# An in-order load queue and accumulating DMA for the weight sums of a Strassen-like up-projection

## The chip, the cores and the metric

One core of a Trainium2 chip runs the whole kernel. The metric is the device time of one execution in microseconds (us), lower is better. TensorE (PE) multiplies, VectorE (DVE) and ScalarE (ACT) prepare operands and take results away, GpSimd (POOL) here does nothing but issue transfers, and SyncE (SP) issues most loads and stores. Each engine works through its own list of instructions in order; waits between engines and transfers are semaphores.

## The reference, cut to what matters

One layer of a decoder on 512 tokens of width 2048, in float32: sliding-window attention with sinks, then a gated feed-forward network with a causal convolution of width 3. The change lies in the second part:

```python
u = h @ w_up                       # 512 x 2048 by 2048 x 11264
c = conv_w[0] * up[:, 0:S] + conv_w[1] * up[:, 1:1 + S] + conv_w[2] * up[:, 2:2 + S]
gate, val = jnp.split(c, 2, axis=-1)
return (jax.nn.silu(gate) * val) @ w_down      # 512 x 5632 by 5632 x 2048
```

## The kernel before, in words

Every float32 operand is split in two float32r halves, high and low: ACT copies the tile to `wh` (line 64), DVE subtracts that from the tile to get `wl` (line 65). Each product is then three matmuls (`prod`, line 83 records them all): high by high, high by low, low by high.

The up-projection works on the 44 column blocks of 128 gate columns and the 128 value columns that belong to them. Blocks 0 to 3 are done in the plain way. Blocks 4 to 43 are done by `up_pair(f)`, in which a 2 by 2 product costs seven block products in place of eight (Winograd's form of Strassen's method). The four weight blocks of a pair, `b11`, `b21`, `b12`, `b22` (512 KB each), come through `block` (line 656) into the pool `bw` of six buffers. DVE forms sums of them in the tile `t` (named `raw`; lines 681, 688, 692, 695). Each of the seven products is 8 x 3 = 24 matmuls of 128x256, so one pair has 168. The order of the products is 2, 7, 5, 6, 3, 1, 4; product 2 needs `b11 + b21`. After the last product ACT copies the result from PSUM (line 704), `gate` does the convolution (lines 567 to 569), SiLU (574) and the gating product (576), and a store on the SP queue writes the activations of the block to the DRAM tensor `hd` (line 578).

The down-projection is also done with seven products. It needs sums of the weight blocks of `wdn`, kept in the DRAM tensor `td`: four sums for each of 22 pairs of blocks (`kp`). The first six are made earlier. The sixteen for `kp` 6 to 21 are made in the up-projection stage, in turn by two helpers that share four buffers `ts` of 512 KB: `weight_sums` (POOL issues four loads, line 141; DVE adds, line 144; POOL issues four stores, line 145) and `queue_sums` (POOL issues loads, line 151, transfers that add to what is in the buffer, line 152, and stores, line 153). Every fifth pair starts one of each kind.

In the down-projection `weight_form` loads 512 KB per step on the SP queue (line 768), from `td` or from `wdn`, into four buffers `raw`; `fetch` (line 555) brings the activations back from `hd`. Each step is 12 matmuls of 128x512, and there are 7 x 22 = 154 steps.

Order: matmuls are pinned to the order of the program text by `tc.keep_in_program_order`. That call orders an instruction behind the one that the text puts last before it on the same engine, whether that one is pinned or not; it sets the order of issue and waits for nothing to finish. All other instructions, the transfers on SP among them, are ordered by a scheduler that works from its own model of the times.

The text around the change reads, in `up_pair` and `gate`:

```python
b11, b21 = block(f, 0, 0), block(f, 1, 0)
...
gate(f, (ug, uv))
...
cv = conv_half(o[1], f, 1)
nc.vector.tensor_tensor(cv, cg, cv, ALU.mult)
nc.sync.dma_start(hd[:, par, :, kp, :].rearrange("m p t -> p m t"), ...)
```

Of the kernel before, what the change touches and what calls it, by code (L numbers as in the profile page):

```python
# [14 lines left out]
ALU = mybir.AluOpType  # L15
# [20 lines left out]
NP = NF // 2  # L36
# [5 lines left out]
def trunk(ctx, tc, xT, x, grow, table, onehot, masked, sinks, conv,  # L42
          wkv, wq, wo, wup, wdn, out):
    nc = tc.nc
# [12 lines left out]
    def bank(i):  # L57
        return ps.tile([P, 512], F32, name=f"b{i}", bufs=1)
# [4 lines left out]
    def split(hi, lo, src):  # L63
        nc.scalar.activation(hi, src, AF.Copy)  # L64
        nc.vector.tensor_tensor(lo, src, hi.bitcast(F32), ALU.subtract)  # L65

    def halves():
        p = ring["slots"][ring["next"] % len(ring["slots"])]
        ring["next"] += 1
        return p.tile([P, 1024], F32R, name="wh"), p.tile([P, 1024], F32R, name="wl")  # L70
# [64 lines left out]
    hd = dr.tile([2, 2, P, NP, HALF], F32, name="hd")  # L135
    td = dr.tile([NP, P, 4, 1024], F32, name="td")

    def weight_sums(kp, sums):
        t = [sums.tile([P, 1024], F32, name="ts") for _ in range(4)]
        for q in (0, 2, 1, 3):  # L140
            nc.gpsimd.dma_start(t[q], wdn[4 * kp + q])
        yield
        for q, o in ((2, 0), (0, 1), (1, 2), (3, 1)):
            nc.vector.tensor_tensor(t[q], t[q], t[o], ALU.add)  # L144
            nc.gpsimd.dma_start(td[kp, :, q, :], t[q])
            yield

    def queue_sums(kp, sums):
        t = [sums.tile([P, 1024], F32, name="ts") for _ in range(4)]
        for q, other in ((2, 0), (0, 1), (1, 2), (3, 1)):  # L150
            nc.gpsimd.dma_start(t[q], wdn[4 * kp + q])
            nc.gpsimd.dma_start(t[q], wdn[4 * kp + other] if q in (0, 2) else t[other], accum_op=ALU.add)
            nc.gpsimd.dma_start(td[kp, :, q, :], t[q])

    def step(g, n=1):
        for _ in range(n):
            next(g, None)

    with ExitStack() as att:
# [10 lines left out]
        with ExitStack() as ph:  # L170
# [26 lines left out]
            for kt in range(KT):  # L197
                if kt == 0:
                    for h in range(2):
                        r = first[:, KT:] if h == 0 else pa.tile([P, 512], F32, name="xs")  # L200
                        c = KT + h * S
                        nc.sync.dma_start(r if h else first, xT[:, c if h else 0:c + S])
                        if h == 0:
                            w = halves()
                            raw = wraw.tile([P, 1024], F32, name="raw")
# [4 lines left out]
                elif kt % 2 == 0:  # L210
                    r = pa.tile([P, 1024], F32, name="xr")
# [205 lines left out]
        for u in range(NKV * NT):  # L417
            t = Unit(u)
# [28 lines left out]
    with ExitStack() as op:  # L447
        sums = op.enter_context(pool("tso", 4))
# [5 lines left out]
        g1 = gp.tile([P, D], F32, name="g1")  # L454
# [42 lines left out]
        def oproj(d, o):  # L497
            for u in range(8):
                w = weights(wo, 8 * d + u)
                for b in range(NT):  # L500
                    for k in range(2):
                        kt = 2 * u + k
                        prod(o[b], station(b, kt), wide(w, k), kt == 0, kt == KT - 1)
                if u % 4 == 0:
                    g = weight_sums(2 * d - 2 + u // 4, sums)
                step(g, (1, 0, 2, 3)[u % 4])
            for b in range(NT):
                evac_m(b, d, o[b])
# [9 lines left out]
        for b, bk in enumerate((2, 5, 6, 7)):  # L518
            o = bank(bk)
            for kt in range(KT):  # L520
                prod(o, station(b, kt), wide(ws[kt // 2], kt % 2), kt == 0, kt == KT - 1)
                if b > 1:
                    turn_tok(b - 2, kt, (0, 1, 3, 4))
                if b < 2:
                    if kt == 0:
                        g = weight_sums(4 + b, sums)
                    if kt in (0, 9, 11, 13, 15):
                        step(g)
            evac_m(b, 3, o)
            xn[b] = finish_tok(b)  # L530

        wu = {(h, u): weights(wup, 2 * h + u) for h in range(4) for u in range(2)}
        o = [bank(k) for k in (0, 1, 2, 5)]
# [18 lines left out]

    def fetch(m, par, g0, g1):
        t, k0 = next((t, k) for t, k, k1 in hq[m, par] if k <= g0 < k1)
        nc.sync.dma_start(t[:, g0 - k0:g1 - k0, :], hd[m, par, :, g0:g1, :])

    with ExitStack() as us:
        fp = us.enter_context(pool("fp", 1))
# [13 lines left out]
        def gate(f, o):  # L572
            cg = conv_half(o[0], f, 0)
            nc.scalar.activation(cg, cg, AF.Silu)
            cv = conv_half(o[1], f, 1)
            nc.vector.tensor_tensor(cv, cg, cv, ALU.mult)
            kp, par = divmod(f, 2)
            nc.sync.dma_start(hd[:, par, :, kp, :].rearrange("m p t -> p m t"),
                              cv.rearrange("p (m t) -> p m t", m=2))
# [72 lines left out]
        sums = tsu.enter_context(pool("tsu", 4, side="right"))  # L652

        def block(f, r, c):
            t = bw.tile([P, 1024], F32, name="bw")
            nc.sync.dma_start(t, wup[4 * f + 2 * c + r])
            return t

        def form(t):
            w = halves()  # L660
            split(*w, t)
            return w

        def times(o, n, w, fresh):
            o3 = o[:, :HALF].rearrange("p (a b) -> p a b", a=2)
            a = forms[n]
            for k in range(8):
                prod(o3, cols(w, k), tuple(v[:, :, k, :] for v in a), fresh and k == 0, k == 7, not fresh)

        def shot(o, name):  # L670
            t = un.tile([P, HALF], F32, name=name)
            nc.scalar.activation(t, o[:, :HALF], AF.Copy)  # L672
            return t

        def up_pair(f, g):
            X, Y, Z = (bank(k) for k in ((0, 1, 6), (3, 4, 7))[f % 2])
            ug = un.tile([P, S], F32, name="ug", bufs=2)
            uv = un.tile([P, S], F32, name="uv", bufs=2)
            b11, b21 = block(f, 0, 0), block(f, 1, 0)
            t = wraw.tile([P, 1024], F32, name="raw")  # L680
            nc.vector.tensor_tensor(t, b11, b21, ALU.add)
            times(X, 2, form(t), True)
            s1 = shot(X, "s1")
            step(g)
            b12 = block(f, 0, 1)
            times(Z, 7, form(b12), True)
            s7 = shot(Z, "s7")
            nc.vector.tensor_tensor(t, t, b12, ALU.add)
            times(X, 5, form(t), False)
            s2 = shot(X, "s2")  # L690
            step(g)
            nc.vector.tensor_tensor(b11, b11, b12, ALU.add)
            times(Z, 6, form(b11), False)
            b22 = block(f, 1, 1)
            nc.vector.tensor_tensor(t, t, b22, ALU.add)
            times(X, 3, form(t), False)
            s3 = shot(X, "s3")
            step(g)
            nc.vector.tensor_tensor(ug[:, :HALF], Z[:, :HALF], s2, ALU.subtract)
            times(Y, 1, form(b21), True)  # L700
            nc.vector.tensor_tensor(uv[:, :HALF], s3, s7, ALU.subtract)
            times(X, 4, form(b22), False)
            nc.vector.tensor_tensor(ug[:, HALF:], s1, Y[:, :HALF], ALU.subtract)
            nc.scalar.activation(uv[:, HALF:], X[:, :HALF], AF.Copy, scale=-1.0)
            gate(f, (ug, uv))

        kp = 6
        for f in range(4, NF):
            i = f - 4
            if i % 5 == 0 and kp < NP:  # L710
                work = weight_sums(kp, sums)
                step(work)
                kp += 1
            up_pair(f, work if i % 5 == 1 else iter(()))
            if i % 5 == 1:
                step(work)
            if i % 5 == 1 and kp < NP:
                queue_sums(kp, sums)
                kp += 1
            if kp == NP and tsu:  # L720
                tsu.close()
                tsu = None
                early = ctx.enter_context(pool("early", 1, side="right"))
                hq[1, 0] = [(early.tile([P, 16, HALF], F32, name="hq10"), 0, 16)]
                for g0, g1 in batches[:4]:
                    fetch(1, 0, g0, g1)
# [38 lines left out]
    def weight_form(src, kp):  # L765
        raw = raws[kp % 2].tile([P, 1024], F32, name="raw")
        table, q = src
        nc.sync.dma_start(raw, td[kp, :, q, :] if table else wdn[4 * kp + q])
        hi, lo = halves()
        split(hi, lo, raw)  # L770
        return hi, lo
# [33 lines left out]
    sums = {}  # L805
# [121 lines left out]
```

## Time and profile before

| | |
|---|---|
| median of 3 runs | 1918.01 us (1916.22 to 1918.19) |
| profiled execution | 1915.05 us, of which 1913.3 us is the span from first to last instruction |
| mean granted TensorE clock | 0.989 |
| PE busy | 1862.9 us, 97% of the span |
| DVE busy | 1455.1 us, 76% |
| bytes moved by DMA | 392.02 MB, 205 GB/s |

The 1.75 us between the span and the time of the execution lie outside of what the profile shows. PE is the busiest engine; a busy PE is one with a matmul under way, whatever its clock. Idle time of another engine costs nothing by itself. The stages can be told apart by what PE multiplies: up to about 380 us projections and attention, then the output projection, then the plain blocks, the 40 pairs of the up-projection (the third product of the first starts at 629.6 us, the last product ends at 1458.4 us), and then the down-projection.

### The profile page before, as it was taken

Reading aid. Unit: us, or ns where it says so; the run is one execution under the profiler, and the core shown is the slowest. Engines: PE = TensorE matmul, PEld = TensorE weight load, DVE = VectorE, ACT = ScalarE, POOL = GpSimd, SP = SyncE. Lnnn points to the kernel's source line nnn. Section 1 sums busy time; section 2 is a strip of 40 time slices with the busy share of each in tenths; the row PEclk is TensorE's granted clock in tenths of the full one; section 3 lists DMA queues with packets and bytes.
Section 4 is the critical chain, followed back from the end, with each engine's and each line's share of the span. In section 5 each row is a group of like instructions: output and inputs, shape, how many; then the busy total and the mean of one; then the engine's idle time right before and its main releaser. Section 6 shows DMA issues by size and latency. Waiting matters only on the chain.

```text
span 1913.3 us, 30053 instructions
## 1 busy us (share of the span) xinstructions
PE 1862.9 (97%) x11822; PEld 1689.4 (88%) x11822; DVE 1455.1 (76%) x2047; ACT 980.9 (51%) x1566; POOL 125.9 (7%) x216
## 2 busy tenths in 40 slices
PE   9999999999999999999999999999996899999998
PEld 7888888888899999998999999999996788888886
DVE  5468888745788979987898988888885466666875
ACT  7357777622344535444454555555553455545553
POOL 0000000012100222222222000000000000000000
PEclk9999999999999999999999999999998999999999
DMA  9533234499643889999999443333335766676773
GB/s 312 149 97 102 93 113 158 144 344 337 242 165 127 273 280 321 304 312 301 329 306 303 166 127 111 126 124 112 127 99 214 261 196 202 189 234 192 236 249 119
DMA packets 120845, 392.02 MB, mean 205 GB/s; under 512 B 13216, under 2 KB 26752, under 8 KB 118784
## 3 DMA queue, kind: packets, MB, share of 16 engines
q1 hardware_dynamic: 86720, 271.84, 42.2%
q0 software_dynamic: 29952, 109.07, 17.8%
q10 hardware_dynamic: 4032, 9.21, 1.6%
q8 instruction: 92, 1.51, 0.3%
q14 instruction: 49, 0.40, 0.1%
HBM read 309.29 MB, written 72.39 MB: 199 GB/s over the span
## 4 chain that ended last, share of the span: by engine, by line
PE 68%; DMA 16%; issue 9%; DVE 6%; ACT 1%; POOL 1%; DVEq 0%; SPq 0%; ACTq 0%; POOLq 0%
PE b L83 66%; DMA ts<-in_wdn 4%; DMA bw<-in_wup 3%; DMA ts<-ts 2%; DVE wl L65 2%; DMA raw<-in_wo 2%; PE b L86 1%; DMA td<-ts 1%; ACT wh L64 1%; DVE ts L144 1%; DMA hq<-hd 1%; DMA raw<-td 0%; DMA raw<-in_wup 0%; DVE xt L482 0%; DVE c L569 0%
## 5 line engine op out<-in xcount | busy, mean ns | idle before, releaser
L64 ACT ACTIVATE wh<-raw 128x1024 fp32r<-128x1024 f32 (+1 forms) x371 | 388.2, 1055 | 489.9 <-PE b L83 267.4
L65 DVE TENSOR_TENSOR wl<-raw,wh 128x1024 fp32r<-128x1024 f32 (+1 forms) x371 | 449.3, 1219 | 231.7 <-ACT wh L64 231.0
L83 PE MATMUL b<-ah,wh 128*128 128x256 f32 (+1 forms) x1824 | 561.9, 308 | 0.9 <-ACT s L672 0.5
L83 PE MATMUL b<-ah,wl 128*128 128x256 f32 (+1 forms) x1824 | 555.8, 305 | 5.9 <-DVE wl L65 5.9
L83 PE MATMUL b<-al,wh 128*128 128x256 f32 (+1 forms) x1824 | 554.4, 304 | 0.4 <-DVE al L65 0.4
L83 PEld LDWEIGHTS b<-ah,wl 128*128 128x128 f32 x1824 | 348.8, 191 | 22.3 <-DVE wl L65 7.7
L83 PEld LDWEIGHTS b<-ah,wh 128*128 128x128 f32 x1824 | 349.3, 192 | 13.2 <-ACT wh L64 2.0
L83 PEld LDWEIGHTS b<-al,wh 128*128 128x128 f32 x1824 | 349.4, 192 | 11.0 <-DVE al L65 0.6
L83 PE MATMUL b<-wh 128*128 128x512 f32 x616 | 241.7, 392 | 19.9 <-ACT wh L64 19.4
L83 PE MATMUL b<-wl,wh 128*128 128x512 f32 x616 | 241.9, 393 | 1.2 <-DVE wl L65 1.2
L83 PE MATMUL b<-wh,wl 128*128 128x512 f32 x616 | 241.4, 392 | 0.0
L64 ACT ACTIVATE wh<-bw 128x1024 fp32r<-128x1024 f32 x160 | 167.6, 1055 | 120.4 <-PE b L83 120.3
L65 DVE TENSOR_TENSOR wl<-bw,wh 128x1024 fp32r<-128x1024 f32 x160 | 194.3, 1219 | 7.6 <-ACT wh L64 7.0
L83 PEld LDWEIGHTS b<-wh 128*128 128x128 f32 x616 | 116.8, 190 | 45.6 <-ACT wh L64 20.3
L83 PEld LDWEIGHTS b<-wl,wh 128*128 128x128 f32 x616 | 116.7, 189 | 26.3 <-DVE wl L65 2.0
L83 PEld LDWEIGHTS b<-wh,wl 128*128 128x128 f32 x616 | 116.8, 190 | 24.2
L83 PE MATMUL b<-wh,ah 128*128 128x512 f32 x320 | 126.5, 395 | 0.0
L83 PE MATMUL b<-wh,al 128*128 128x512 f32 x320 | 124.8, 390 | 0.0
L83 PE MATMUL b<-wl,ah 128*128 128x512 f32 x320 | 124.6, 389 | 0.0
L144 DVE TENSOR_TENSOR ts<-ts 128x1024 f32<-128x1024 f32 x56 | 68.4, 1221 | 40.2 <-DMA ts<-in_wdn 31.8
L672 ACT ACTIVATE s<-b 128x256 f32<-128x256 f32 x160 | 59.3, 371 | 73.9 <-PE b L83 73.9
L83 PE MATMUL b<-f6h,wh 128*128 128x256 f32 x320 | 92.3, 288 | 5.0 <-ACT s L672 5.0
(165 smaller groups left out, 3099.4 us busy)
## 6 DMA issues: line engine op xcount, KB each, us to landing
bw<-in_wup SPq DMA_DIRECT2D x160, 512.0 KB, 4.8
ts<-in_wdn POOLq DMA_DIRECT2D x104, 512.0 KB, 8.3
td<-ts POOLq DMA_DIRECT2D x88, 512.0 KB, 5.5
raw<-td SPq DMA_DIRECT2D x88, 512.0 KB, 4.7
raw<-in_wdn SPq DMA_DIRECT2D x66, 512.0 KB, 4.2
raw<-in_wq SPq DMA_DIRECT2D x32, 512.0 KB, 3.6
raw<-in_wo SPq DMA_DIRECT2D x32, 512.0 KB, 4.8
hd<-c SPq DMA_DIRECT2D x44, 256.0 KB, 4.5
```

The lines of the kernel that those rows point to most:

```text
L64: nc.scalar.activation(hi, src, AF.Copy)
L65: nc.vector.tensor_tensor(lo, src, hi.bitcast(F32), ALU.subtract)
L83: tc.keep_in_program_order(nc.tensor.matmul(o, l, r, start=start, stop=stop, skip_group_check=more))
L86: tc.keep_in_program_order(nc.tensor.transpose(o, src, ident))
L144: nc.vector.tensor_tensor(t[q], t[q], t[o], ALU.add)
L672: nc.scalar.activation(t, o[:, :HALF], AF.Copy)
```

## The change

The loads of the weight blocks of the pairs, of the sums' inputs, of the down-projection's weights and of its activations are pinned on the SP queue in the order of the text. All sixteen weight sums of the stage are made by `queue_sums`, whose four loads move from POOL to SP; DVE no longer adds any of them. They are started ahead of the pairs with `i % 9` in 0, 2, 4, 6, which spreads them over 34 of the 40 pairs. The store to `hd` in `gate` is left as it was: on SP, and not itself pinned.

```diff
+    def in_turn(o, i):
+        tc.keep_in_program_order(nc.sync.dma_start(o, i))
...
     def queue_sums(kp, sums):
         t = [sums.tile([P, 1024], F32, name="ts") for _ in range(4)]
-        for q, other in ((2, 0), (0, 1), (1, 2), (3, 1)):
-            nc.gpsimd.dma_start(t[q], wdn[4 * kp + q])
-            nc.gpsimd.dma_start(t[q], wdn[4 * kp + other] if q in (0, 2) else t[other], accum_op=ALU.add)
+        for q in (2, 0, 1, 3):
+            in_turn(t[q], wdn[4 * kp + q])
+
+        def add(q, o):
+            nc.gpsimd.dma_start(t[q], o, accum_op=ALU.add)
+
+        def store(q):
             nc.gpsimd.dma_start(td[kp, :, q, :], t[q])
+
+        add(2, wdn[4 * kp])
+        add(0, wdn[4 * kp + 1])
+        store(2)
+        add(1, t[2])
+        store(0)
+        add(3, t[1])
+        store(1)
+        store(3)
...
     def fetch(m, par, g0, g1):
-        nc.sync.dma_start(t[:, g0 - k0:g1 - k0, :], hd[m, par, :, g0:g1, :])
+        in_turn(t[:, g0 - k0:g1 - k0, :], hd[m, par, :, g0:g1, :])
...
         def block(f, r, c):
-            nc.sync.dma_start(t, wup[4 * f + 2 * c + r])
+            in_turn(t, wup[4 * f + 2 * c + r])
...
-        def up_pair(f, g):
+        def up_pair(f):
...
         for f in range(4, NF):
             i = f - 4
-            if i % 5 == 0 and kp < NP:
-                work = weight_sums(kp, sums)
-                step(work)
-                kp += 1
-            up_pair(f, work if i % 5 == 1 else iter(()))
-            if i % 5 == 1:
-                step(work)
-            if i % 5 == 1 and kp < NP:
+            if i % 9 in (0, 2, 4, 6) and kp < NP:
                 queue_sums(kp, sums)
                 kp += 1
+            up_pair(f)
...
     def weight_form(src, kp):
-        nc.sync.dma_start(raw, td[kp, :, q, :] if table else wdn[4 * kp + q])
+        in_turn(raw, td[kp, :, q, :] if table else wdn[4 * kp + q])
```

The three calls of `step(g)` inside `up_pair`, which let DVE add the sums between the products, go as well.

## Rows read from the trace of the kernel before

**Rows 1.** Windows: length; PE, PEld, DVE, ACT, POOL busy; PEclk; DMA share; GB/s.

```profile
690.00:750.00 60.00, 55.84 (x441) 55.43 (x440) 55.41 (x62) 28.42 (x42) 12.98 (x22) 0.94 0.92 301
...
1150.00:1250.00 100.00, 100.00 (x836) 100.00 (x835) 85.67 (x95) 53.77 (x75) 0.00 (x0) 1.00 0.39 125
```

**Rows 2.** Tile `f5h`, the third product of each pair: first and last start.

```profile
L83 PE MATMUL b<-f5h,wh x320: 277/283/416, 629.6 to 1446.4; 128*128 128x256 f32 x160
```

**Rows 3.** Timeline of PE: the last matmul of the last pair; start, us.

```profile
1458.16 0.28 PE L83 MATMUL b<-f4h,wl 128*128 128x256 f32 x1
```

**Rows 4.** Timeline of the SP queue from 1415 us; start, us, line, transfer.

```profile
1418.85 0.33 SPq L656 DMA_DIRECT2D bw<-in_wup  x1
...
1424.72 0.38 SPq L578 DMA_DIRECT2D hd<-c  x1
...
1444.03 0.37 SPq L578 DMA_DIRECT2D hd<-c  x1
...
1463.17 0.38 SPq L578 DMA_DIRECT2D hd<-c  x1
```

**Rows 5.** Waits of the SP queue, whole span: us in total, times, longest.

```profile
SPq L656 <- DVE wl L65: 605.9, 132, 12.8
...
SPq L578 <- DVE c L576: 50.7, 38, 3.7
```

**Rows 6.** Timeline of ACT behind the last pair.

```profile
1458.51 0.36 ACT L704 ACTIVATE uv<-b 128x256 f32<-128x256 f32 x1
1458.90 0.72 ACT L567 ACTIVATE c<-uv,cw 128x512 f32<-128x512 f32 x1
```

**Rows 7.** Timeline of DVE behind the last pair.

```profile
1458.88 1.22 DVE L65 TENSOR_TENSOR wl<-raw,wh 128x1024 fp32r<-128x1024 f32 x1
...
1460.67 0.74 DVE L568 SCALAR_TENSOR_TENSOR c<-uv,cw,c 128x511 f32<-128x511 f32 x1
...
1462.31 0.69 DVE L576 TENSOR_TENSOR c<-c,c 128x512 f32<-128x512 f32 x1
```

**Rows 8.** DMA issues, 1100 to 1440 us: count, size, median us to landing.

```profile
bw<-in_wup SPq DMA_DIRECT2D x64, 512.0 KB, 3.6
hd<-c SPq DMA_DIRECT2D x17, 256.0 KB, 3.1
```

**Rows 9.** DMA issues, 640 to 1060 us.

```profile
bw<-in_wup SPq DMA_DIRECT2D x78, 512.0 KB, 7.2
ts<-in_wdn POOLq DMA_DIRECT2D x76, 512.0 KB, 8.3
td<-ts POOLq DMA_DIRECT2D x63, 512.0 KB, 6.3
ts<-ts POOLq DMA_DIRECT2D x16, 512.0 KB, 8.5
```

**Rows 10.** Chain that ended last, from a load to the matmul; start, us, what.

```profile
1485.09 8.97 DMA raw<-td
1495.17 1.24 DVE wl L65
1496.45 408.21 PE b L83 x1787
```

**Rows 11.** Windows around two pauses of PE (near 696 and 1495 us).

```profile
698.00:700.00 2.00, 2.00 (x11) 2.00 (x11) 2.00 (x3) 1.26 (x3) 0.25 (x1) 0.50 0.41 166
...
1486.00:1490.00 4.00, 4.00 (x19) 3.33 (x18) 0.00 (x0) 0.00 (x0) 0.00 (x0) 1.00 1.03 409
...
1496.00:1498.00 2.00, 1.55 (x4) 1.27 (x5) 0.59 (x2) 1.28 (x2) 0.00 (x0) 0.50 0.47 125
...
1502.00:1504.00 2.00, 2.00 (x9) 1.56 (x9) 1.57 (x2) 0.96 (x1) 0.00 (x0) 0.87 0.66 166
```

**Rows 12.** Waits of PE from 630 to 1500 us: us in total, times, longest.

```profile
PE b L83 <- ACT wh L64: 19.8, 3, 15.4
```

**Rows 13.** Tile `bw`: the first sum of a pair (min/median/max ns).

```profile
L681 DVE TENSOR_TENSOR raw<-bw x40: 1214/1218/1227, 609.8 to 1410.5; 128x1024 f32<-128x1024 f32 x40
```

More of the change, by code (lines that the diff above doesn't have):

```diff
@@ L683, in up_pair @@
             s1 = shot(X, "s1")
-            step(g)
             b12 = block(f, 0, 1)
@@ L690, in up_pair @@
             s2 = shot(X, "s2")
-            step(g)
             nc.vector.tensor_tensor(b11, b11, b12, ALU.add)
@@ L697, in up_pair @@
             s3 = shot(X, "s3")
-            step(g)
             nc.vector.tensor_tensor(ug[:, :HALF], Z[:, :HALF], s2, ALU.subtract)
```

## The prediction

> **What bounds the kernel now.** I read the page first: PE is busy for nearly all of the span, so a change off PE can win only what PE loses in pauses, and can cost far more if it makes new ones. Next the windows of the up-projection stage, since the change is there. One early and one late stretch stand in [rows 1]. In the late one PE is never idle and starts 836 matmuls in 100 us, 0.1196 us each, so a pair of 168 takes 20.1 us; DMA is busy for 0.39 of the time. In the early one, where the sums are made, DMA is busy for 0.92 and PE loses time. To size that loss: the third product of the first pair starts at 629.6 us [rows 2], two products of 24 matmuls earlier is 623.9, and the last matmul ends at 1458.4 [rows 3]. That is 834.5 us for 40 pairs; 40 x 20.1 is 804. So the stage loses about 30 us, and this is all that a better flow of loads could win there. Behind the stage PE waits another 19.8 us in three waits for weights, the longest 15.4 [rows 12].
>
> Last I read why the loads are in time today: the timeline of the SP queue. The last weight block of the last pair is issued at 1418.85 us, before the stores of the last three pairs (1424.72, 1444.03 and 1463.17) [rows 4]. The scheduler thus lets the loads run two stores ahead of the text, as far as the six buffers go. The waits of the queue say the same: the loads of line 656 wait 605.9 us in total for DVE to free a buffer, that is, they are ready long before they are needed. The store of line 578 waits too, 50.7 us in 38 places, for DVE's gating product [rows 5].
>
> **The change part by part.** The pin orders each load behind the last SP instruction ahead of it in the text. For `b11` of a pair that instruction is the `hd` store of the pair before it, or, where sums start, the four loads of `queue_sums`, the first of which stands behind that store. The store itself isn't pinned, but nothing pinned behind it can pass it, and it needs the end of its own pair: last product, copy, convolution, gating. So no weight of a pair can be asked for until the pair before it is finished and gated, and PE has nothing to do meanwhile: its matmuls are pinned, and the first product needs `b11` and `b21`. The six buffers are of no use any more. The pause, step by step:
>
> (a) Last matmul to the store's issue. After the last pair the copy starts 0.07 us behind the last matmul, and ACT's convolution step ends at 1459.62 [rows 3, 6]. DVE could go on at 1459.66 but had a split of another tile and a step of the gate half ahead of it until 1460.67; from there to the store's issue at 1463.17 it is 2.5 us [rows 4, 7]. Without the other tiles, which won't be there to split, 1459.66 + 2.5 = 1462.16, that is 3.7 us behind the last matmul. The row as it stands is 4.7. I take 3.7, since in the changed kernel DVE's next split waits for a load.
>
> (b) Store, `b11`, `b21`. The issue takes 0.38 us [rows 4]; a 512 KB load in the stretch without sums lands 3.6 us after its issue [rows 8]. `b21` follows; 409 GB/s are moved where the SP queue alone is at work [rows 11], so its 512 KB take 1.3 us more, and the 256 KB of the store ahead up to 0.6. Together 5.3 to 5.9; I take 5.6. The lower bound is 5.0, the upper one is from the stretch with the sums, where a load takes 7.2 [rows 9]: 0.4 + 7.2 + 512 KB at 301 GB/s [rows 1] = 9.3. The stretch without sums is nearer, as most of a pair's own POOL traffic is over when the next pause comes.
>
> The Trainium skill has a fit for this (DMA: Bandwidth & Descriptors, Anatomy of one DMA, for transfers issued from GpSimd): 2.0 us and the bytes over 436 GB/s, so 3.2 us for such a load where the row shows 3.6. With the store and both loads in line it gives an estimate of 5.4 us, and the sum below would be some 8 us less.
>
> (c) Landing to the first matmul. The sum `b11 + b21` takes 1.22 us on DVE [rows 13]. Then the split: in the chain a load landed at 1485.09 + 8.97 = 1494.06 us and PE started at 1496.45, 2.4 us later [rows 10]. With the hand-over 3.7.
>
> The pause is 3.7 + 5.6 + 3.7 = 13.0 us. (d) It also costs clock. After a pause the granted clock stood at 0.50, the 1.2 GHz level: from 1496 to 1502 us and around 698 [rows 11], where 11 matmuls fall in 2 us; full clock gives 836 / 50 = 17 [rows 1]. Full clock was back in the window from 1502 to 1504. About 5.6 us at half speed lose 2.8 us; bounds 2.3 and 3.0. So 15.8 us a pair, 632 us for 40.
>
> (e) Sixteen pairs start with the four loads of the sums, 2.1 MB ahead of `b11` on the same queue. At 409 GB/s that is 5.1 us; at half of the 301 GB/s of the mixed stretch [rows 1], if POOL's adds take the other half, 13.9. The adds can start only when the first `ts` has landed, so I take 8: 128 us. The bounds give 82 and 222.
>
> (f) DVE loses the adds of half the sums and POOL's load issues become SP's; both engines have slack in these pauses, so nothing. The bytes of the sums grow, as all 16 now add by transfer (4 loads, 4 adds and 4 stores of 512 KB each), but are spread over a stage that is nearly twice as long: no saturation is left, and the 30 us that PE loses today go with it (bounds 20 and 30).
>
> (g) The down-projection starts on the same rule: its first weight load goes out behind the last `hd` store but ahead of every fetch that is still to come, where today fetches stand in front. Its pause is 3.7 + 0.4 + 3.6 + 2.4 = 10.1, with the clock 12.9; today 19.8 us of waits [rows 12] and two stretches at half clock, 25.4. A gain of 12, bounds 0 and 20. Further on a step of 12 matmuls outlasts its load as it does now, and the fetches come in the text well before their use: nothing.
>
> Sum: 632 + 128 - 30 - 12 = 718 us on the profiled execution's 1915 (its span of 1913.3 and 1.75 around it), so 2633; that execution is 3 us under the median of the runs shown. I say 2635. All lower bounds together: 40 x (3.7 + 5.0 + 3.6 + 2.3) = 584, and 82, less 30 and 20: 2531. All upper ones: 40 x (4.7 + 9.3 + 3.7 + 3.0) = 828, and 222, less 20: 2945.
>
> **The rivals.** *Faster: the store doesn't hold the loads.* Were it issued late, as today, or held aside while the queue goes on, the six buffers would still cover the loads. The sums would then need 4 x 6.3 MB in nine pairs of 20.1 us, 139 GB/s, with the 125 of [rows 1] 264 against the 301 of the mixed stretch. The 30 us in the stage and 12 behind it would be won in whole or half: 1873 to 1894. It decides at one point: whether a load can leave the SP queue while an earlier store waits. For it speaks that today's loads do run ahead; against it that they do so by standing ahead in the queue [rows 4], and that the queue itself is seen waiting at the store [rows 5]. The Trainium skill says (DMA: Bandwidth & Descriptors, Anatomy of one DMA) that a transfer's wait is done by the issuing sequencer before dispatch, not by the DMA engines; by that rule the loads are held, and the wait at line 578 agrees.
>
> *Slower still: the sums' buffers hold the queue too.* A set's chain is a load, three adds in line and a store: 8.3 + 3 x 8.5 + 6.3 = 40 us by the busy rows [rows 9]. The next set starts two pairs later, 2 x 36 = 72 us. Only a chain over 72 us makes the loads of `ts`, and all behind them, wait; at twice the busy rows, 80 us, this costs 16 x 8 = 128 us more: 2760.
>
> *No change:* the scheduler's order was the text's already. [Rows 4] says no: 1915.
>
> **How the numbers follow.** Forecast 0.86, faster 0.09, buffers 0.04, no change 0.01. The range must leave out the fast rival and little more: 2500, just below the lower bounds, to 2800, which takes in the buffer rival and upper bounds of some terms, as all at once is unlikely. A difference within 0.2% (4 us) can't be told from none here: faster 0.09, same 0.01, slower 0.90.
>
> **What would show it.** In the trace after: on the SP queue each `hd` store directly ahead of the four loads of the next pair (with four `ts` loads between them sixteen times); 40 pauses of PE of about 13 us, some 8 more in sixteen of them, each followed by 5 to 6 us at clock 0.50; PE's share of the span near 75%; waits of line 656 for buffers gone, and waits of line 578 for `c` grown to hundreds of us; the stage some 1560 us long. Wrong would be: loads of a pair issued before the store of the pair ahead; pauses that are short because the load lands in 2 us; or a POOL chain that outlasts two pairs.

## The result, and the profile after

The changed kernel takes 2671.41 us (2670.0 to 2674.39) against 1918.1 us before: a ratio of 1.393, 95% interval 1.391 to 1.396. The forecast was 2635 us, with a range of 2500 to 2800. The profiled execution took 2674.39 us, of which the span is 2672.5; the span before was 1913.3, so 759.2 us have to be found. (Lines of the kernel moved by 16: `gate`'s store is line 594, the split is still 64 and 65, and all pinned loads of the new helper are recorded at line 139.)

The page comes first: the busy row of PE, and the chain that ended last.

```profile
PE 1970.5 (74%) x11822; PEld 1778.9 (67%) x11822; DVE 1447.3 (54%) x2015; ACT 981.8 (37%) x1566; POOL 120.7 (5%) x184
...
PEclk9999999998677687786776877877868788999999
...
PE b L83 70%; DMA bw<-in_wup 13%; SPq L139 2%; DVE wl L65 2%; DVE bw L706 2%; PE b L86 1%; DVE c L585 1%; DVE c L584 1%; DVE c L592 1%; DVE raw L697 1%; ACT c L590 1%; ACT c L583 1%; SPq L594 1%; ACT wh L64 0%; DMA raw<-in_wkv 0%
```

PE's work is the same 11822 matmuls, its share of the span falls from 97% to 74%, and the clock row has dents from a fourth to five sixths of the span: that is the stage of the pairs. The chain shows what sets the end besides PE: the loads of `bw`, 13%, and then, 1% to 2% each, the steps of the gate (583 to 592), the store (594) and the split, that is, the whole path from the end of one pair to the start of the next.

Where the stage begins and ends is read as in [rows 2, 3], from tile `f5h` and the last matmul:

```profile
L83 PE MATMUL b<-f5h,wh x320: 280/283/287, 653.5 to 2218.6; 128*128 128x256 f32 x160
```

```profile
2230.36 0.28 PE L83 MATMUL b<-f4h,wl 128*128 128x256 f32 x1
```

From the third product of the first pair to that of the last it is 1565.1 us, before 816.8. From the start of the last matmul to the end of the span it is 442.1 us, before 455.1 [rows 3]. So the loss is all in the pairs, and the down-projection gained 13.0.

One pause without sums, then one with, on the SP queue (start, us, line, transfer, count):

```profile
1039.35 0.38 SPq L594 DMA_DIRECT2D hd<-c  x1
1039.82 1.86 SPq L139 DMA_DIRECT2D bw<-in_wup  x4
1075.36 0.38 SPq L594 DMA_DIRECT2D hd<-c  x1
1075.84 1.86 SPq L139 DMA_DIRECT2D ts<-in_wdn  x4
1077.79 2.31 SPq L139 DMA_DIRECT2D bw<-in_wup  x4
```

The four loads of a pair stand directly behind the store of the pair ahead, where [rows 4] had them two stores earlier; where sums start, the `ts` loads stand between. This is so at 38 of the 40 pairs. At two the pin did not keep the order that the text says. Ahead of the first pair the `ts` loads and `b11` went out (626.17 and 627.98 us) before the store of the block ahead (628.52). And in the pair behind the last sums, where the text also has the first four fetches of `hq`, the queue reads (1940 to 2075 us)

```profile
1980.62 2.75 SPq L139 DMA_DIRECT2D bw<-in_wup  x4
2010.89 1.75 SPq L139 DMA_DIRECT2D hq<-hd  x4
2012.75 2.16 SPq L139 DMA_DIRECT2D bw<-in_wup  x4
2029.00 24.96 SPq L594 DMA_DIRECT2D hd<-c  x2
```

The fetches and the next pair's loads passed the store at 2029.00, and the pause there was 5.3 us. No run shows why the pin did not hold at these two places. The waits of the queue (us in total, times, longest) say what it waited for:

```profile
SPq L594 <- DVE c L592: 1454.0, 43, 42.5
```

Before, the queue waited 50.7 us there, and 605.9 us for free buffers [rows 5]. The same pause seen from DVE and from PE:

```profile
1038.63 0.69 DVE L592 TENSOR_TENSOR c<-c,c 128x512 f32<-128x512 f32 x1
1045.86 1.23 DVE L697 TENSOR_TENSOR raw<-bw 128x1024 f32<-128x1024 f32 x1 [6.53 <-DMA bw<-in_wup]
1047.16 1.23 DVE L706 TENSOR_TENSOR bw<-bw 128x1024 f32<-128x1024 f32 x1
1048.30 1.22 DVE L65 TENSOR_TENSOR wl<-raw,wh 128x1024 fp32r<-128x1024 f32 x1
```

```profile
1035.20 0.28 PE L83 MATMUL b<-f4h,wl 128*128 128x256 f32 x1
1048.22 0.58 PE L83 MATMUL b<-ah,wh 128*128 128x256 f32 x1 [12.75 <-ACT wh L64]
...
1049.58 0.58 PE L83 MATMUL b<-ah,wl 128*128 128x256 f32 x1 [0.55 <-DVE wl L65]
```

The chain that ended last has the landing of `b21`:

```profile
1040.33 5.43 DMA bw<-in_wup
```

The last matmul ends at 1035.48, the store goes out at 1039.35, `b21` is there at 1045.76, and the first matmul that needs the low half (`wl`) runs at 1049.58: 14.1 us. The clock behind the pause (columns as in [rows 1]):

```profile
1050.00:1052.00 2.00, 2.00 (x11) 2.00 (x11) 1.79 (x2) 0.17 (x1) 0.00 (x0) 0.50 0.00 0
1052.00:1054.00 2.00, 2.00 (x16) 2.00 (x15) 1.09 (x1) 1.89 (x3) 0.00 (x0) 0.79 0.00 0
1054.00:1056.00 2.00, 2.00 (x19) 2.00 (x18) 2.00 (x3) 0.33 (x1) 0.00 (x0) 1.00 0.00 0
```

And all pauses together, waits of PE from 640 to 2235 us:

```profile
PE b L83 <- ACT wh L64: 639.4, 41, 23.6
PE b L83 <- DVE wl L65: 46.1, 40, 3.1
```

That is 685.5 us. Some 4 of them are the down-projection's first wait, so 681 are the 40 pauses of the pairs. Counted as above, to the first matmul that needs the low half, the pauses come to 714: PE runs two matmuls a little earlier, at half clock, and the waits leave that time out. By this count the PE timeline has 23 pauses without sums of 13.4 to 14.9 us (median 13.9), 15 with sums of 23.4 to 25.0 (median 24.3), the first of 22.4 and the short one of 5.3.

### The profile page after: what moved, and what is told of

The parts are those of the page before. It is cut to its first block, busy times and chain, and to the rows that moved or that the text cites. A ratio compares the mean times of both kernels' runs of the same rounds, so it can differ in the third digit from the quotient of the medians.

```text
span 2672.5 us, 29978 instructions
## 1 busy us (share of the span) xinstructions
PE 1970.5 (74%) x11822; PEld 1778.9 (67%) x11822; DVE 1447.3 (54%) x2015; ACT 981.8 (37%) x1566; POOL 120.7 (5%) x184
## 4 chain that ended last, share of the span: by engine, by line
PE 71%; DMA 14%; DVE 8%; SPq 3%; ACT 2%; issue 2%; DVEq 0%; ACTq 0%
PE b L83 70%; DMA bw<-in_wup 13%; SPq L139 2%; DVE wl L65 2%; DVE bw L706 2%; PE b L86 1%; DVE c L585 1%; DVE c L584 1%; DVE c L592 1%; DVE raw L697 1%; ACT c L590 1%; ACT c L583 1%; SPq L594 1%; ACT wh L64 0%; DMA raw<-in_wkv 0%
## 5 line engine op out<-in xcount | busy, mean ns | idle before, releaser
L83 PE MATMUL b<-ah,wh 128*128 128x256 f32 (+1 forms) x1824 | 610.2, 335 | 636.4 <-ACT wh L64 636.4
L83 PEld LDWEIGHTS b<-ah,wh 128*128 128x128 f32 x1824 | 393.4, 216 | 656.2 <-ACT wh L64 645.7
L83 PE MATMUL b<-ah,wl 128*128 128x256 f32 (+1 forms) x1824 | 600.8, 329 | 46.4 <-DVE wl L65 46.3
L83 PE MATMUL b<-al,wh 128*128 128x256 f32 (+1 forms) x1824 | 594.9, 326 | 0.4 <-DVE al L65 0.4
L83 PEld LDWEIGHTS b<-ah,wl 128*128 128x128 f32 x1824 | 389.4, 213 | 73.4 <-DVE wl L65 58.8
L83 PEld LDWEIGHTS b<-al,wh 128*128 128x128 f32 x1824 | 393.3, 216 | 11.0 <-DVE al L65 0.6
L697 DVE TENSOR_TENSOR raw<-bw 128x1024 f32<-128x1024 f32 x40 | 49.0, 1225 | 390.9 <-DMA bw<-in_wup 390.9
```

The source lines that it names most:

```text
L83: tc.keep_in_program_order(nc.tensor.matmul(o, l, r, start=start, stop=stop, skip_group_check=more))
```

## The experiments

The theory is that the store to `hd`, unpinned but standing in the text between one pair's loads and the next, holds the SP queue. One rival is that the sixteen sums by adding transfers cost the time (16.8 MB more, chains on POOL); another that any fixed order of the loads does. All times below were taken beside the kernel before on the same chip (1917 to 1919 us).

**e1: the store on another queue.** The changed kernel with

```diff
-            nc.sync.dma_start(hd[:, par, :, kp, :].rearrange("m p t -> p m t"),
+            nc.scalar.dma_start(hd[:, par, :, kp, :].rearrange("m p t -> p m t"),
```

> The changed kernel with one edit: the store to hd is issued by ACT, so it is no longer in the SP queue ahead of the next pair's loads. If that store is what holds the loads, the 40 pauses of 14 to 24 us go (685 us of waits in the profile of the changed kernel, and 120 us at half clock), the loads run ahead by six buffers again, and the time is 1870 to 1900. If the adding transfers of the sums are the cost (16.8 MB more, and chains on POOL), it stays above 2500. If any fixed order of the SP loads is the cost, it stays above 2500 too.

Measured: 1913.29 us, 0.997 of before (0.996 to 0.998). One instruction on another queue takes 758 us away, with all pins and all sums left in place; both rivals fall as the cause of the loss. It is 13 us above the expected range. The waits of PE from 640 to 1475 us show why not less:

```profile
PE b L83 <- ACT wh L64: 20.2, 1, 20.2
PE b L83 <- ACT s L688: 11.1, 18, 1.6
```

A single wait of 20.2 us ahead of the first pair: there the first `ts` load waits on the SP queue for its buffer (36.4 us, until DVE's `al` of line 617), and the pair's loads are pinned behind it.

**e2: the pair's loads free.** The changed kernel with

```diff
-            in_turn(t, wup[4 * f + 2 * c + r])
+            nc.sync.dma_start(t, wup[4 * f + 2 * c + r])
```

> The changed kernel with the pin taken off the loads of bw alone; the loads of ts, raw and hq stay pinned. If the store holds the loads: the scheduler lets bw run ahead as before and the pauses go, 1870 to 1910. The loads of ts may still stand behind a store, which holds back nothing that PE needs soon. If the sums are the cost: above 2500.

Measured: 1885.44 us, 0.982 of before (0.979 to 0.986), as expected, and the fastest kernel of all. The same pin on `ts`, `raw` and `hq` does no harm.

**e3: the next pair's loads ahead of the gate in the text.** All pins kept, the store too:

```diff
+        def blocks(f):
+            return [block(f, r, c) for c in range(2) for r in range(2)] if f < NF else None
...
+            ahead = blocks(f + 1)
             gate(f, (ug, uv))
+            return ahead
```

> The changed kernel, all pins kept, but the four block loads of the next pair stand in the text ahead of the gate (and its store) of the pair. If the store's place is the cause, this gives the loads a lead of some 16 us over their use and the pauses go: 1870 to 1900. If pinned loads as such are the cost, or the sums, it stays above 2500.

Measured: 2089.33 us (ratio 1.085 to 1.093). The cause is right by its size, 582 us won by moving four calls; the expected time was missed by 190 us. The SP queue, and PE's windows of the same stretch, show what was forgotten:

```profile
947.32 0.38 SPq L594 DMA_DIRECT2D hd<-c  x1
947.79 3.88 SPq L139 DMA_DIRECT2D bw<-in_wup  x4
974.87 0.38 SPq L594 DMA_DIRECT2D hd<-c  x1
975.67 1.76 SPq L139 DMA_DIRECT2D ts<-in_wdn  x4
977.53 2.63 SPq L139 DMA_DIRECT2D bw<-in_wup  x4
```

```profile
980.00:985.00 5.00, 5.00 (x44) 5.00 (x43) 2.02 (x4) 0.81 (x2) 1.80 (x2) 1.00 1.04 383
985.00:990.00 5.00, 0.41 (x4) 0.21 (x2) 1.08 (x2) 1.51 (x3) 0.23 (x1) 0.92 1.03 267
990.00:995.00 5.00, 0.48 (x2) 0.48 (x2) 2.61 (x3) 1.59 (x2) 1.78 (x3) 0.50 1.04 329
```

A pair's loads stand behind the store of the pair before the last, and that store is now late: while loads are at hand, the scheduler lets DVE split for the next pair before it finishes the gate, so the queue still waits 724 us for `c` (640 to 1640 us). Where sums start, 2.1 MB go ahead as well; the loads issued at 977.5 come too late for the pair that PE would start at 985.

**e4: no pins at all.** The changed kernel with a plain load in `in_turn`:

```diff
-        tc.keep_in_program_order(nc.sync.dma_start(o, i))
+        nc.sync.dma_start(o, i)
```

> The changed kernel with no pin on any load; what is left of the change is the sixteen sums by adding transfers, spread over 34 pairs, with their loads on SP in the scheduler's order. If the pins behind the store are the whole loss: 1870 to 1910, that is, the sums alone win part of the 30 us that PE lost in the stage before. If the sums are the loss: above 2500.

Measured: 1896.34 us, 0.988 of before (0.985 to 0.992). What is left of the change without its pins (the sums by adding transfers, their loads on SP) wins time. The pairs end 22 us earlier than before (their last matmul starts at 1436.2 in place of 1458.2 us); the down-projection starts as badly as before.

**e5: the pin on the pair's loads alone, in the kernel before.**

```diff
-            nc.sync.dma_start(t, wup[4 * f + 2 * c + r])
+            tc.keep_in_program_order(nc.sync.dma_start(t, wup[4 * f + 2 * c + r]))
```

> The kernel before with one edit: the loads of bw are pinned, nothing else is changed, the sums are made as before. If the store ahead of the pinned loads is the loss: 40 pauses of 14 us and 3 us of half clock each, less the 30 us that the stage lost before: 1918 + 650, so 2530 to 2600. If it takes the sums on the SP queue too to lose the time, it stays below 2200.

Measured: 2574.54 us (ratio 1.339 to 1.344), in the range. This one pin is enough for 655 of the 753 us. Here no `ts` load stands in the SP queue, and yet eight of the pauses, early in the stage, have waits of 18 to 23 us, while POOL's transfers for the sums run beside. One of them:

```profile
851.55 0.58 PE L83 MATMUL b<-ah,wh 128*128 128x256 f32 x1 [21.88 <-ACT wh L64]
```

**e6: the sums' loads behind the pair's own.** The changed kernel, with `queue_sums` called inside `up_pair` behind `b22 = block(f, 1, 1)`.

> The changed kernel, but the four loads of ts stand in the text behind the pair's own four loads in place of ahead of them. If the sixteen longer pauses (22 to 24 us against 14) are the 2.1 MB in front of b11: they shrink to 14 us, 16 x 9.5 = 150 us less, 2500 to 2540. If the POOL transfers that go on beside are what lengthens them: less than 50 us are won, above 2620.

Measured: 2510.17 us, 161 less than the changed kernel, 10.1 for each set of sums. PE's waits from 640 to 2065 us:

```profile
PE b L83 <- ACT wh L64: 488.6, 39, 13.5
```

The longest is 13.5 us, where it was 23.6. The edit moves two things out of the pause, the 2.1 MB ahead of `b11` and POOL's first adds, which follow these loads at once. In the trace of the changed kernel, by the median of 15 pauses, the four `ts` loads land 4.4, 6.4, 7.7 and 9.0 us behind the store and `b21` at 15.3; without sums it is there at 6.3. Four loads 1.3 us apart make some 5 of these 9 us. The other 4 pass while the first adds are under way:

```profile
1080.64 0.91 POOL L157 DMA_DIRECT2D ts<-in_wdn  x1 [59.55 <-DMA ts<-in_wdn]
1082.23 0.91 POOL L157 DMA_DIRECT2D ts<-in_wdn  x1 [0.68 <-DMA ts<-in_wdn]
```

The long pauses of e5 speak for the adds' share too; no run takes out the one without the other.

**e7: matmuls in the pauses.** The changed kernel with extra matmuls into a bank that nobody reads; extra work, to see what the clock costs.

```diff
             gate(f, (ug, uv))
+            fill(0 if f == NF - 1 else 105 if (f - 3) % 9 not in (0, 2, 4, 6) or kp >= NP else 185)
...
+        def fill(n):
+            for j in range(n):
+                h = forms[4][0]
+                mm(i3, h[:, 0, j % 8, :], h[:, :, j % 8, :], True, True)
```

> The changed kernel with extra matmuls that nobody reads, 105 behind each pair but the last, 185 where the next pair starts sums, meant to take less than the pause (12.5 of 14 us, 22 of 24 us at full clock). The loads are as late as before. If the pause costs clock as the rows say, PE starts the next pair at full speed and 2.5 to 3 us are saved at each of 39 pauses: 2550 to 2580. If the slow start behind a pause has another cause (operands that come late one by one), the time stays at 2671 or grows.

Measured: 2621.65 us. 5295 matmuls more, and 50 us less: half of what was expected. Mean clock in the stage, by the windows of this kernel and then of the changed one:

```profile
700.00:2180.00 1480.00, 1419.34 (x11589) 1407.88 (x11589) 678.18 (x724) 401.95 (x572) 86.64 (x120) 0.99 0.41 127
```

```profile
700.00:2220.00 1520.00, 871.20 (x6334) 850.61 (x6333) 675.81 (x720) 403.87 (x569) 86.64 (x120) 0.76 0.39 123
```

The half clock is gone (0.99 for 0.76). In a stretch without sums one pair lasts 34.2 us (from the matmul that waited at 1005.41 to that at 1039.64) where it was 36.9 (1012.68 to 1049.58): 2.7 us saved. From the first matmul that needs the low half to the end of the pair's last, the median pair takes 22.3 us in the changed kernel and 20.2 here, so half clock costs 2.1 us a pair, less than the 2.5 to 3 expected. Over the 39 hand-overs between pairs the matmuls are some 70 us shorter and the pauses some 20 longer, 7 of these in the pause that was short before (12.7 for 5.3). Why the others grew is not settled.

**e8: both moves of e3 and e6.** The next pair's loads ahead of the gate, the `ts` loads behind them.

> As e3_hoist (the next pair's four loads stand in the text ahead of the gate), and the loads of ts stand behind them in place of ahead. The pauses left in e3_hoist were 17, about one for each set of sums. If they were the 2.1 MB of ts ahead of the next pair's loads, they go: 1880 to 1920. If the hoist by one pair is too short by itself, because the store waits for a gate that DVE does late, pauses stay in most pairs and the time is above 2000.

Measured: 1972.85 us (ratio 1.026 to 1.031). Between the two expectations: the `ts` loads were 116 of the 171 us that e3 lost to the kernel before, but 55 remain. The store still waits 654 us for `c`, and PE has small waits in many pairs, as a lead of one pair that is too short would make. But one pair alone takes 37.9 us in place of 20.2: the one ahead of which the fetches of `hq` stand, with a pause of 14.1.

**e9: the pins on the down-projection's loads alone, in the kernel before** (`fetch` and `weight_form`).

> The kernel before with the pins on the down-projection's loads alone (raw and hq); the pairs and the sums stay as they were. If the better start of the down-projection (13 us from the last matmul of the pairs to the end in the profile of the changed kernel) is a matter of these pins: 1903 to 1908. If it came from the sums or from a calmer DMA: 1916 to 1920.

Measured: 1903.36 us, 0.992 of before (0.990 to 0.995): 15 us less, as expected of the pins. In its trace 441.8 us lie between the start of the pairs' last matmul and the end of the span, as in the changed kernel (442.1).

**e10: e1 with the sums' loads behind the pair's own.**

> As e1_store_act (the store to hd issued by ACT), and the loads of ts stand in the text behind the pair's own loads. In e1_store_act PE waited 20.2 us once, ahead of the first pair, where the first ts load waited for its buffer and the pair's loads stood behind it. If that is what e1 still lost: 1885 to 1895. If the ACT queue, now held at the store, is what it lost: 1908 to 1916.

Measured: 1905.67 us (ratio 0.992 to 0.996), between the two. The first pair comes 12.5 us earlier than in e1 (third product at 640.3 in place of 652.8), but its 39 pairs take 809.1 us where e2's take 796.2. Of these 13 us 8.8 are one pair's (29.8 for 21.0), behind the last sums. The longest wait for the sums' stores on the SP queue, and the issues behind it (1280 to 1370 us):

```profile
SPq L139 <- DMA td<-ts: 35.8, 3, 27.4
```

```profile
1323.75 1.75 SPq L139 DMA_DIRECT2D hq<-hd  x4
1325.55 37.24 SPq L139 DMA_DIRECT2D bw<-in_wup  x12
```

The pinned fetches waited 27.4 us for the stores of the sums, the next pair's loads stood behind them, and PE paused for 6.0 us. So most of the 13 us is not the store on ACT's queue but the same thing again, pinned loads behind a transfer that waits. The first pair still starts 11.0 us later than in e2 (629.3).

**e11: all sums added on DVE**, no pins, the kernel before otherwise; fewer bytes than before.

```diff
-            if i % 5 == 0 and kp < NP:
+            if i % 5 in (0, 2) and kp < NP:
...
-            up_pair(f, work if i % 5 == 1 else iter(()))
+            up_pair(f, work if i % 5 in (1, 3) else iter(()))
```

> The kernel before, no pins, but all sixteen sets of sums are added on DVE (weight_sums), none by adding transfers; started at pairs with i % 5 of 0 and 2. In e4_no_pins, where none is added on DVE, DMA is busy for 0.9 and more of the same 400 us (323 GB/s) and yet PE loses almost nothing in the pairs; so the 30 us that the stage lost before may be due not to the full DMA but to DVE's adds, which wait in DVE's queue for their loads. By that, twice as many such adds lose more: 1930 to 1950. If the full DMA is the cause, the 17 MB fewer that this moves win time: 1895 to 1912.

Measured: 1937.86 us (ratio 1.009 to 1.012). Three windows of one stretch, 640 to 1060 us, tell the two causes apart: e4 (no adds on DVE), the kernel before (half), e11 (all), in this order.

```profile
640.00:1060.00 420.00, 416.71 (x3453) 415.70 (x3452) 352.64 (x394) 220.89 (x310) 80.24 (x112) 1.00 1.03 323
```

```profile
640.00:1060.00 420.00, 401.75 (x3275) 398.61 (x3273) 363.96 (x402) 203.88 (x294) 94.98 (x155) 0.98 0.95 307
```

```profile
640.00:1060.00 420.00, 386.32 (x3102) 380.53 (x3101) 385.19 (x416) 193.66 (x278) 65.69 (x123) 0.98 0.77 263
```

PE is idle for 3, 18 and 34 us, while DMA is busy for 1.03, 0.95 and 0.77. The fuller the DMA, the less PE loses; the more adds on DVE (none, 31 and 63 in this stretch, 0, 37.8 and 76.9 us of its time), the more. In the kernel before, one such add can be followed to PE:

```profile
900.53 1.23 DVE L144 TENSOR_TENSOR ts<-ts 128x1024 f32<-128x1024 f32 x1 [2.54 <-DMA ts<-in_wdn]
901.67 1.22 DVE L688 TENSOR_TENSOR raw<-raw,bw 128x1024 f32<-128x1024 f32 x1
902.98 1.06 ACT L64 ACTIVATE wh<-raw 128x1024 fp32r<-128x1024 f32 x1 [8.92 <-DVE raw L688]
906.94 0.39 PE L83 MATMUL b<-f5h,wh 128*128 128x256 f32 x1 [1.79 <-ACT s L672]
```

The add held DVE until its load was there, the pair's own sum came behind it, ACT waited for that sum before it could copy a product away, and PE paused 1.8 us before 906.94 for that copy.

## Why the prediction was right, point by point

**The mechanism.** The store heads the queue and the pinned loads don't pass it: seen on the SP queue at 38 of 40 pairs, and shown by e1 (the store moved: 758 us back) and e5 (one pin: 655 us lost). The Trainium skill's rule (DMA: Bandwidth & Descriptors, Anatomy of one DMA), that the issuing sequencer does the waiting before dispatch, agrees with the trace: 1454.0 us of waits at line 594. The first of the 40 pauses is another: its `ts` load waited 21.0 us for a buffer.

**The sizes.** Predicted and measured, in us (medians, where a term comes many times):

| term | predicted | measured |
|---|---|---|
| (a) last matmul to the store | 3.7 | 3.9 |
| (b) store to `b21` landed | 5.6 | 6.3 |
| (c) landed to matmuls at work | 3.7 | 3.8 |
| pause without sums | 13.0 | 13.9 |
| (e) more, for each set of sums | 8 | 10.4; 10.1 by e6 |
| 40 pauses | 648 | 714 |
| (d) half clock, a pair | 2.8 | 2.1 (e7); 2.2 from what is left of the stage |
| (f) the old loss of the stage | -30 | gone: 0.3 of waits outside the pauses |
| (g) start of the down-projection | -12 | -13.0 |

The stage lasts from 623.8 to 2230.6, 1606.8 us; less 804 of work and 714 of pauses leaves 89 at half clock. 714 + 89 - 30 - 13 = 760 accounts for the span to 1 us. The forecast had 648 + 112 - 30 - 12 = 718. That it came within 2% is in part luck: the forecast had the pauses 66 us too short and the half clock 23 us too long. Most of the 66 is (e), about 50 in 15 sets, for which the prediction took 8 out of bounds of 5.1 to 13.9; the ordinary pauses make about 22, and the pause in which the loads passed the store gives 8 back. In (b), `b11` lands 4.8 us behind the store's issue, where the prediction's 0.4 + 3.6 make 4.0 and its 0.6 for the bytes of the store 4.6 at most, and `b21` 1.5 behind it, where it had 1.3. Why they are later no run shows. In (d) the prediction took 5.6 us at half clock from two pauses; behind the 38 pauses of 13 us and more between the pairs it is 3.0 to 6.2 us from the first matmul that needs the low half, median 5.0.

In (g) the three waits of [rows 12] aren't all behind the stage: 0.4 us of the 19.8 lies in it. That changes nothing in the sum.

**Right in number, wrong in reason: (f).** "No saturation is left, and the 30 us that PE loses today go with it." The loss did go, but it was never the full DMA: e4 keeps DMA at 1.03 of that stretch and loses 3 us, e11 has it at 0.77 and loses 34. It went with DVE's adds, which the forecast put at nothing because of DVE's slack.

**The rivals.** The fast one (store not holding the loads, 1873 to 1894) is what e2 measures, 1885; its price was right and its condition wasn't met. The buffers of `ts` held the queue ahead of the first pair, and behind the last sums, where the fetches of `hq` waited 24.6 us for the stores of the sums. The first cost a long pause that the forecast had anyway (22.4 for 21.0), the second a pause of 5.3, as the loads passed the store there.

## What to carry to other kernels

A pin is meant to order an instruction behind whatever stands ahead of it on the same queue (here it did at 38 of 40 pairs), and a store that waits for the end of an iteration turns a pinned queue into a barrier: before pinning loads, list what else is in that queue and what it waits for (here the store, and in e10 the fetches), and put it elsewhere or leave those loads free. Where some loads do better pinned and others don't, pin them one by one: here the pins behind the stage (15 us) and the sums by transfer (22 us) were gains that one pin in front buried under some 700. A loss in a stretch where DMA is full isn't thereby DMA's; take the engine's work out and see.

## What the runs showed of the hardware that was not expected

DMA engines at 1.03 of a stretch and 323 GB/s, with the queue for weights among them, left PE idle for 3 us of 420 as long as the loads ran ahead. And the clock came back to full level 3.0 to 6.2 us after work began again behind each long pause between the pairs, whether the pause lasted 14 us or 24, so that forty pauses cost 89 us of clock beside 714 us of waiting.
